# State space steps issued singly between weight pieces, tables through the weight pool, next layer's parameters begun inside the gated unit

## The chip, the cores and the metric

The kernel runs as one program on one core of a Trainium2 chip. Its time is the device time of one execution in microseconds (us), as the median of several executions. The core's engines run side by side and meet only through semaphores: TensorE (PE) does the matrix products, VectorE (DVE), ScalarE (ACT) and GpSimd (POOL) do elementwise work, and SyncE (SP) issues nearly all of this kernel's DMA transfers, in one queue, in program order. Every engine works through its own instructions strictly in order, so an instruction that waits holds up all that stand behind it on that engine.

## The reference

The input is one sequence of 512 positions with 2048 features. Two layers of the same kind follow one another and then a third block of another kind (a gated delta rule beside a sliding window attention), which the change does not touch. One of the first two layers, cut to what matters:

```python
mod = c_act @ w_ada[l] + b_ada[l]                  # 6144 numbers: shift, scale, gate
h = rms_norm(x, norm_g[l]) * (1 + scale) + shift
u, z_s, q, k, v, z_a = split(h @ w_in[l])
y_s = s5_mixer(u, ...) * silu(z_s)
y_a = diff_attention(rope(q), rope(k), v, ...) * silu(z_a)      # 8 heads, two score maps each
x = x + gate * (concatenate([y_s, y_a]) @ w_out[l])

def s5_mixer(u):                                   # 64 groups of 16 channels, 64 complex states each
    a_bar = exp(lam * step); b_bar = (a_bar - 1) / lam * b_mat
    states = scan(a_bar, b_bar @ u)                # linear recurrence over the 512 positions
    y = gelu(real(c_mat @ states) + d_skip * u)
    ab = y @ w_glu + b_glu
    return ab[:, :1024] * sigmoid(ab[:, 1024:])
```

All data are fp32.

## The kernel before, in words

**Weights.** Every weight comes in pieces of 128 x 1024 fp32 (512 KB). `piece` (lines 258 to 274) loads one into a slot of the pool `rawp`, which has five; ACT rounds it into a `hi` part (L266) and `raw - hi` becomes the `lo` part (L269), each in a pool of three slots. `mm3` multiplies in three passes: hi by the activations' high part (`HH`, L281), hi by their low part (`HL`, L282), lo by the high part (L284). For a 128 x 1024 piece against 512 positions that is 24 matmuls. `group_tok` does the same with the activations as the stationary side (L353 to L355), for the values of the attention. `self.pool` decides which engine makes `lo`: with `pool = 2`, which `layer` sets for the attention heads 2 to 7, every second piece's `lo` is made by GpSimd, otherwise all by DVE.

**Filling in.** `mod` of the coming layer is computed without PE: an "ada" piece of `w_ada` is loaded into a slot of the same five (L531) and DVE multiplies and sums it at once (L517, the "dot"). `piece` adds `self.rate` to a counter and calls `self.fill` for each whole number, so that 0.75 or 1 ada piece goes with each weight piece.

**A layer's stages.** `layer(l)` makes u and the gates z_a; then the values of heads 0 to 3 (`group_tok` over eight pieces); heads 0 to 3 (each two weight blocks of two pieces, for q and k, then `attention`); the values of heads 4 to 7; heads 4 to 7; z_s; the gated linear unit `glu` (16 pieces, 8 pairs m of a gate block and a value block); and the out projection (`woA` by `group` in 8 pieces, then `wo` block by block). The stages begin roughly at 315, 385, 775, 880 and 1060 us for layer 0's values, heads, `glu`, out projection and layer 1, and at 1290 and 1345 us for layer 1's values and heads; the third block fills the time from 1960 us on.

**The state space part.** `ssm_params(l)` is a generator that computes tables from the parameters: `prep` builds powers E for a quarter of the states on DVE (`powmul`, L659 to L661: three tensor_tensor operations for each power and part, up to 128 x 512), `products` (L688) and `turned` (L718) multiply and transpose E on PE and write the tables `FT_d`, `K_d` to DRAM, `carried` builds powers on GpSimd and writes `CA_d`. Layer 1's generator, `par_next`, is stepped during layer 0's out projection: first once after `glu`, then from the third `woA` piece on at each piece and after each `wo` block. `ssm_steps(l)` is a generator of 16 loads of u, 8 steps with the tables `FT` (L806, sixteen 64 x 64 matmuls each), the recurrence on GpSimd (62 steps of four small operations, L818 to L821), and 8 steps with `K_d`, `CA_d` and the states (L844, L846). The FT table of step q is loaded as two 256 KB transfers (L799) into one of two halves of the upper part of A, which also receives the values of heads 4 to 7 later. `layer` steps this generator in runs: in layer 0 four steps after the first values and then 4, 4 and 5 in heads 0 and 1; in layer 1 5 and 4 in head 0; and one step after each weight block of heads 4 to 7.

**What sets the order.** The program is written in the order of these calls; a scheduler of the framework then sets each engine's order by priorities and readiness in its own model, and the pools decide which slot an instruction must wait for. `later(600)` gives the recurrence a later priority. DMAs stand in SP's queue in the scheduled order: a load whose slot is still in use holds all later loads.

Of the kernel before, what the change touches and what calls it, by code (L numbers as in the profile page):

```python
# [167 lines left out]
class Kern:  # L168
    def __init__(self, ctx, tc, I, O):
# [18 lines left out]
        self.turn = self.pool = 0  # L188
# [70 lines left out]
    def piece(self, src, n=1024):  # L259
        nc = self.nc  # L260
        self.n_ = getattr(self, "n_", 0) + 1
        raw = self.rawp.tile([128, 1024], F32, tag="raw", name=f"raw_{self.n_}")
        hi = self.hip.tile([128, 1024], F32, tag="hi", name=f"hi_{self.n_}")
        lo = self.lop.tile([128, 1024], F32, tag="lo", name=f"lo_{self.n_}")
        nc.sync.dma_start(raw[:, :n], src)
        nc.scalar.copy(hi[:, :n].bitcast(F32R), raw[:, :n])  # L266
        self.turn = (self.turn + 1) % 4
        eng = nc.gpsimd if self.turn < self.pool else nc.vector
        eng.tensor_tensor(lo[:, :n].bitcast(F32R), raw[:, :n], hi[:, :n], SUB)  # L269
        self.due += self.rate  # L270
# [15 lines left out]
    def blocks(self, srcs, acts, evac, pair=False):  # L286
# [13 lines left out]
        for j, src in enumerate(srcs):  # L300
            ps = self.bank()
            for k0 in range(0, nk, 8):
                hi, lo = self.piece(src[:, k0 * 128:(k0 + 8) * 128])
                self.mm3([(ps, slice(k * 128, (k + 1) * 128), acts[k0 + k], k0 + k == 0, k0 + k == nk - 1) for k in range(8)], hi, lo)
            evac(j, ps)
# [268 lines left out]
    def ssm_params(self, l):  # L574
# [77 lines left out]
        sbqs = [t.rearrange("p (k r a c) -> p k r a c", k=2, r=2, a=8) for t in (g[:, 1536:2048], self.sb2)]  # L652
# [10 lines left out]
        def prep(qd):  # L663
            sbq = sbqs[qd % 2]
# [15 lines left out]
            return E, Cb  # L680

        def products(qd, E, Cb):
# [40 lines left out]
        def carried(qd):  # L723

            sbq = sbqs[qd % 2]
# [11 lines left out]
        for qd in range(4):  # L737
            k = products(qd, *made)
            turned(qd, made[0], (0,))
            yield  # L740
            turned(qd, made[0], (1,))
# [4 lines left out]
            carried(qd)  # L746
# [3 lines left out]
    def ssm_param_storage(self):  # L750
# [10 lines left out]
        self.sb2 = self.small(512, "sb2")  # L761
# [21 lines left out]
    def ssm_steps(self, l):  # L783
# [12 lines left out]
        for q in range(8):  # L796
            ft = self.A[:, 4 + q % 2 * 2:6 + q % 2 * 2, :].rearrange("p a b -> p (a b)")
            for r in range(2):
                nc.sync.dma_start(ft[:, r * 512:(r + 1) * 512], self.FT_d[l][q, r])  # L799
# [69 lines left out]
    def glu(self, l):  # L869
# [8 lines left out]
        for m in range(8):  # L878
# [11 lines left out]
            self.blocks([wg[m]], acts, ev_a)  # L890
        for m in range(8):
# [103 lines left out]
    def layer(self, l, xsrc, on_x, nxt, after_u=lambda: None, par=iter(()), par_next=iter(())):  # L995
# [33 lines left out]
        self.group_tok(I[f"wv{l}"][0], hacts, 512, lambda t, ps: nc.scalar.copy(va[:, t, :], ps), 0, (beside, lambda: None)[l])  # L1029
        for _ in range((4, 0)[l]):  # L1030
            next(ssm)

        def head(h, vt, side):
            qk = []
            self.pool = 2 if h >= 2 else 0
            for b, n in zip((h, 8 + h), side):
                self.blocks([wi[b]], hacts, lambda j, ps: qk.append(self.rope(ps, "q")))
                for _ in range(n):
                    next(ssm, None)
            self.attention(l, h, qk[0], qk[1], vt)  # L1040
        for h in range(4):
            head(h, va, (((4, 4), (5, 0), (0, 0), (0, 0)), ((5, 4), (0, 0), (0, 0), (0, 0)))[l][h])
        vb = A[:, 4:8, :]
        self.group_tok(I[f"wv{l}"][1], hacts, 512, lambda t, ps: nc.scalar.copy(vb[:, t, :], ps))
        for h in range(4, 8):
            head(h, vb, (1, 1))
        for _ in ssm:
            pass
        self.pool = 0
# [14 lines left out]
        self.glu(l)  # L1064
        self.rate = (1, 1)[l]
        next(par_next, None)
# [12 lines left out]
        wait = iter((0, 0))  # L1079
        self.group([I[f"woA{l}"]], [4], yacts, ev_o, side=lambda: next(par_next, None) if next(wait, 1) else None)  # L1080
# [617 lines left out]
```

## Time and profile before

| | us |
|---|---|
| median of 3 executions (3540.87 to 3544.72) | 3542.14 |
| the profiled execution | 3540.92 |
| its span in the trace | 3538.8 |
| PE busy in that span | 3373.7 |
| DVE busy | 2121.2 |
| ACT busy | 1184.6 |
| GpSimd busy | 631.2 |

The trace covers one execution. Busy time is time in which an engine works on an instruction; idle time has a releaser, which is the event that ended it. Only idle time of the engine that sets the end counts. The table of stretches gives, beside the busy times, the clock that TensorE was granted as a share of full speed: after a pause the engine starts again at the lower of its two levels (1.2 GHz instead of 2.4 GHz), and matmuls then start about twice as far apart. DMA share is the mean busy share of the core's 16 DMA engines.

### The profile page before, as it was taken

To read this page: it belongs to the slowest core of one execution; us is meant where nothing else is said; L and a number is where in the kernel's file an instruction comes from. 1 tells how busy PE (TensorE), PEld (TensorE's weight loads), DVE (VectorE), ACT (ScalarE), POOL (GpSimd) and SP (SyncE) were. 2 spreads that over 40 slices of the span, in tenths; PEclk is the share of its full clock that TensorE was granted. 3 is DMA by queue.
4 is the path that set the end of the run, shared out by engine and by line. 5 is a ranking of instruction groups with operands and counts; after the bars stand their busy time and mean duration, and the time that the engine had idled before them with its cause. 6 is when DMAs were issued, how large, how long until landed. Compare 5 with 4: busy or idle time off the path is not lost.

```text
span 3538.8 us, 45321 instructions
## 1 busy us (share of the span) xinstructions
PE 3373.7 (95%) x16541; PEld 2699.5 (76%) x16541; DVE 2121.2 (60%) x4108; ACT 1184.6 (33%) x2044; POOL 631.2 (18%) x885
## 2 busy tenths in 40 slices
PE   7988989999789998899999998999999999999999
PEld 4867767778669876677788887788888877688887
DVE  7994655677957435646575588933893265434432
ACT  3422332353224322323433344222522244433311
POOL 0083591001830004920001202000200000000000
PEclk9999999999899999999999999999999999999999
DMA  9848436656666855356567636233333232224442
GB/s 333 301 155 227 155 117 185 187 186 210 200 215 221 231 172 164 111 174 183 176 220 232 203 118 133 100 107 93 104 96 115 94 107 75 75 99 139 143 140 90
DMA packets 265116, 565.02 MB, mean 160 GB/s; under 512 B 76732, under 2 KB 113853, under 8 KB 264893
## 3 DMA queue, kind: packets, MB, share of 16 engines
q1 hardware_dynamic: 264894, 562.14, 50.2%
q8 instruction: 130, 2.13, 0.2%
q14 instruction: 92, 0.75, 0.1%
HBM read 497.89 MB, written 50.50 MB: 155 GB/s over the span
## 4 chain that ended last, share of the span: by engine, by line
PE 66%; DVE 10%; DMA 10%; POOL 8%; issue 3%; SPq 2%; ACT 1%; DVEq 0%; POOLq 0%; ACTq 0%
PE pp L282 18%; PE pp L281 18%; PE pp L284 18%; DMA raw<-in_wada 6%; DVE lo L269 2%; PE sc L918 2%; DVE G L249 2%; POOL misc L818 1%; POOL G L821 1%; POOL misc L820 1%; POOL misc L819 1%; DVE raw L517 1%; POOL lo L269 1%; POOL G L661 1%; PE pp L353 1%
## 5 line engine op out<-in xcount | busy, mean ns | idle before, releaser
L281 PE MATMUL pp<-HH,hi 128*128 128x512 f32 (+1 forms) x3568 | 1390.5, 393 | 29.5 <-ACT HH L567 18.4
L282 PE MATMUL pp<-HL,hi 128*128 128x512 f32 (+1 forms) x3440 | 1336.5, 392 | 3.2 <-DVE HL L252 3.2
L266 ACT CAST hi<-raw 128x1024 fp32r<-128x1024 f32 (+1 forms) x538 | 560.1, 1043 | 1173.4 <-PE pp L282 918.7
L284 PE MATMUL pp<-HH,lo 128*128 128x512 f32 (+1 forms) x3568 | 904.4, 391 | 8.9 <-DVE lo L269 8.9
L269 DVE TENSOR_TENSOR lo<-raw,hi 128x1024 fp32r<-128x1024 f32 (+1 forms) x506 | 623.6, 1234 | 356.2 <-PE pp L284 183.5
L281 PEld LDWEIGHTS pp<-HH,hi 128*128 128x128 f32 x3568 | 676.3, 190 | 183.3 <-issue 30.0
L284 PEld LDWEIGHTS pp<-HH,lo 128*128 128x128 f32 x3568 | 658.7, 189 | 162.1 <-issue 20.0
L282 PEld LDWEIGHTS pp<-HL,hi 128*128 128x128 f32 x3440 | 651.9, 190 | 152.6 <-issue 22.5
L517 DVE CUSTOM_DVE_ANT_0 raw<-raw,cs,mod 128x1024 f32<-128x1024 f32 x112 | 154.9, 1383 | 245.7 <-DMA raw<-in_wada 243.0
L517 DVE CUSTOM_DVE_ANT_0 raw<-raw,cs,vec 128x1024 f32<-128x1024 f32 x112 | 153.0, 1366 | 231.5 <-DMA raw<-in_wada 224.8
L217 ACT ACTIVATE p<-p,st 128x128 f32<-128x128 f32 (+2 forms) x192 | 101.9, 531 | 201.1 <-DVE st L244 200.9
L1652 POOL TENSOR_TENSOR rp<-rp,n 128x512 f32<-128x512 f32 (+1 forms) x43 | 59.0, 1385 | 430.9 <-ACT n L1651 430.9
L354 PE MATMUL pp<-lo,HH 128*128 128x512 f32 (+1 forms) x320 | 121.7, 385 | 4.1 <-DVE lo L269 4.1
L353 PE MATMUL pp<-hi,HH 128*128 128x512 f32 (+1 forms) x320 | 121.1, 384 | 4.6 <-ACT HH L567 3.1
L269 POOL TENSOR_TENSOR lo<-raw,hi 128x1024 fp32r<-128x1024 f32 x32 | 78.2, 2443 | 263.0 <-PE pp L284 171.9
L355 PE MATMUL pp<-hi,HL 128*128 128x512 f32 (+1 forms) x320 | 115.4, 381 | 0.0
L818 POOL TENSOR_TENSOR misc<-misc,G 128x64 f32<-128x64 f32 x124 | 57.1, 461 | 310.7 <-ACT G L808 301.5
L918 PE MATMUL sc<-rp,rp 64*128 64x128 f32 (+3 forms) x256 | 92.3, 492 | 9.6 <-DVE st L920 9.6
L282 PE MATMUL pp<-A,hi 128*128 128x512 f32 x256 | 100.7, 393 | 0.0
L920 DVE CUSTOM_DVE_ANT_0 p<-sc,cst 128x128 f32<-128x128 f32 (+3 forms) x128 | 61.1, 484 | 39.3 <-PE sc L918 39.0
L1101 POOL TENSOR_TENSOR wt<-n,wt 128x512 fp32r<-128x512 f32 x16 | 24.7, 1545 | 321.4 <-ACT wt L1100 168.7
L354 PEld LDWEIGHTS pp<-lo,HH 128*128 128x128 f32 x320 | 62.5, 196 | 18.7 <-DVE lo L269 5.8
(327 smaller groups left out, 3911.6 us busy)
## 6 DMA issues: line engine op xcount, KB each, us to landing
raw<-in_wada SPq DMA_DIRECT2D x224, 512.0 KB, 4.1
raw<-in_w SPq DMA_DIRECT2D x164, 512.0 KB, 3.6
raw<-in_win SPq DMA_DIRECT2D x128, 512.0 KB, 5.0
raw<-in_wo SPq DMA_DIRECT2D x80, 512.0 KB, 4.6
G<-in_wad SPq DMA_DIRECT2D x64, 512.0 KB, 6.1
raw<-in_wv SPq DMA_DIRECT2D x32, 512.0 KB, 3.7
raw<-in_wglu SPq DMA_DIRECT2D x32, 512.0 KB, 4.5
raw<-in_wuA SPq DMA_DIRECT2D x18, 512.0 KB, 4.7
```

The source lines that it names most:

```text
L217: i = self.nc.scalar.activation(out, src, func, **kw)
L266: nc.scalar.copy(hi[:, :n].bitcast(F32R), raw[:, :n])
L269: eng.tensor_tensor(lo[:, :n].bitcast(F32R), raw[:, :n], hi[:, :n], SUB)
L281: mm(out, hi[:, sl], mh, start=first, stop=False)
L282: mm(out, hi[:, sl], ml, start=False, stop=False)
L284: mm(out, lo[:, sl], mh, start=False, stop=last)
L353: mm(pss[t][:, :n], mh[:, ts], hi[:, sl], start=first, stop=False)
L354: mm(pss[t][:, :n], mh[:, ts], lo[:, sl], start=False, stop=False)
L355: mm(pss[t][:, :n], ml[:, ts], hi[:, sl], start=False, stop=last)
L517: self.nc.vector.tensor_tensor_reduce(w, w, cs, 1.0, self.vec[:, o:o + 1] if first else m, MUL, ADD, m)
L818: T(s1, a8[:, 0], prev, MUL)
L918: nc.tensor.matmul(sc[:, :W], q[rows, i * 128:(i + 1) * 128], k[rows, :W], start=True, stop=True)
```

## The change

1. **No lo parts on GpSimd.** `self.pool` and `self.turn` go; `piece` makes every `lo` on DVE. This concerns 32 pieces, 16 in each of the two layers, in heads 2 to 7.
2. **State space steps singly.** `blocks` gets a callback `side` after each piece. In layer 0, the counts `(8, 1, 2, 2, 2, 2)` are the steps after the first six pieces of heads 0 and 1 (before: 4 after the values, then 4, 4, 5 after blocks). In layer 1, one step is issued after each of the eight pieces of the first values, which are the eight FT steps, and one (the recurrence) after the first piece of head 0 (before: none beside the values, then 5 and 4 in head 0). Heads 4 to 7 keep one step after each block.
3. **FT tables through the pieces' pool.** An FT step takes a slot of the five raw slots and loads its table with one 512 KB transfer, in place of the two halves in A.
4. **Layer 1's parameters begun in the gated unit.** `glu` gets a callback `beside`, which steps `par_next` after m = 1, 3, 4, 5 and 6; the step after `glu` goes, and in `woA` only the fourth and the eighth piece step it (before: the third to the eighth). The slice of inputs `sbq` moves to the pool `rp` (four slots, shared with rope's tiles) from two fixed places, so `sb2` goes.

The diff, cut to its core:

```diff
@@ piece
-        self.turn = (self.turn + 1) % 4
-        eng = nc.gpsimd if self.turn < self.pool else nc.vector
-        eng.tensor_tensor(lo[:, :n].bitcast(F32R), raw[:, :n], hi[:, :n], SUB)
+        nc.vector.tensor_tensor(lo[:, :n].bitcast(F32R), raw[:, :n], hi[:, :n], SUB)
@@ blocks
-    def blocks(self, srcs, acts, evac, pair=False):
+    def blocks(self, srcs, acts, evac, pair=False, side=lambda: None):
...
+                side()
             evac(j, ps)
@@ ssm_params, prep
-            sbq = sbqs[qd % 2]
+            sbq = self.t2("rp", 4).rearrange("p (k r a c) -> p k r a c", k=2, r=2, a=8)
@@ ssm_steps
-            ft = self.A[:, 4 + q % 2 * 2:6 + q % 2 * 2, :].rearrange("p a b -> p (a b)")
-            for r in range(2):
-                nc.sync.dma_start(ft[:, r * 512:(r + 1) * 512], self.FT_d[l][q, r])
+            ft = self.raw()
+            nc.sync.dma_start(ft.rearrange("p (r c) -> p r c", r=2), self.FT_d[l][q].rearrange("r p c -> p r c"))
@@ glu
-    def glu(self, l):
+    def glu(self, l, beside):
...
             self.blocks([wg[m]], acts, ev_a)
+            if m in (1, 3, 4, 5, 6):
+                beside()
@@ layer
-        self.group_tok(I[f"wv{l}"][0], hacts, 512, ..., 0, (beside, lambda: None)[l])
-        for _ in range((4, 0)[l]):
-            next(ssm)
+        self.group_tok(I[f"wv{l}"][0], hacts, 512, ..., 0, (beside, lambda: next(ssm))[l])
+        steps = iter(((8, 1, 2, 2, 2, 2), (1,))[l])
+        def side():
+            for _ in range(next(steps, 0)):
+                next(ssm)
...
-            self.pool = 2 if h >= 2 else 0
...
-        self.glu(l)
-        next(par_next, None)
+        self.glu(l, lambda: next(par_next, None))
...
-        wait = iter((0, 0))
-        self.group([I[f"woA{l}"]], [4], yacts, ev_o, side=lambda: next(par_next, None) if next(wait, 1) else None)
+        turns = iter((0, 0, 0, 1) * 2)
+        self.group([I[f"woA{l}"]], [4], yacts, ev_o, side=lambda: next(turns) and next(par_next, None))
```

After the change `mm3`'s lines are L278, L279 and L281, the products' L685, the transposes' L715, the FT matmuls' L801, the recurrence's L813 to L816, `powmul`'s L656 to L658, the lo part's L266, the dot's L515, the loads' L264 (weights), L529 (ada) and L794 (FT).

**GpSimd in layer 0's heads.** The engine's own order in the middle of the recurrence, before (`lo_3674` is the low part of a weight piece):

```order
L818 TENSOR_TENSOR misc<-misc,G_90 128x64
L819 TENSOR_TENSOR misc<-misc,G_90 128x64
L820 TENSOR_TENSOR misc<-misc,G_90 128x64
L269 TENSOR_TENSOR lo_3674<-raw_3672,hi_3673 128x1024
L821 TENSOR_TENSOR G_90<-misc 128x64
L818 TENSOR_TENSOR misc<-misc,G_90 128x64
```

and after:

```order
L813 TENSOR_TENSOR misc<-misc,G_90 128x64
L814 TENSOR_TENSOR misc<-misc,G_90 128x64
L815 TENSOR_TENSOR misc<-misc,G_90 128x64
L816 TENSOR_TENSOR G_90<-misc 128x64
L813 TENSOR_TENSOR misc<-misc,G_90 128x64
```

The low part no longer stands between the steps of the recurrence, and no step stands ahead of it.

**SP at layer 1's first values and head 0.** The queue of loads before, from the second piece of head 1 on (`in_win`; the values' pieces `in_wv` stand ten to twenty rows further up, the first four FT halves some ninety):

```order
L265 DMA raw_11138<-in_win 128x1024
L531 DMA raw_11144<-in_wada 128x1024
L799 DMA A_86<-FT_d_134 128x512
L265 DMA raw_11182<-in_win 128x1024
L531 DMA raw_11188<-in_wada 128x1024
L265 DMA raw_11215<-in_win 128x1024
L531 DMA raw_11221<-in_wada 128x1024
L799 DMA A_86<-FT_d_134 128x512
L901 DMA rp_10488<-rp_10487 32x512 x4
L799 DMA A_86<-FT_d_134 128x512 x3
```

and after, from the first piece of the values on:

```order
L264 DMA raw_10168<-in_wv 128x1024
L794 DMA raw_10199<-FT_d_134 128x2x512
L264 DMA raw_10219<-in_wv 128x1024
L529 DMA raw_10225<-in_wada 128x1024
L794 DMA raw_10252<-FT_d_134 128x2x512
L264 DMA raw_10272<-in_wv 128x1024
L529 DMA raw_10278<-in_wada 128x1024
L794 DMA raw_10305<-FT_d_134 128x2x512
```

Each table now has a place directly behind a piece of the values, and takes a raw slot there. PE's order in the same place, before, where the end of the first table's matmuls and the second table stand behind head 0's second piece (`lo_10456`):

```order
L282 MATMUL pp_10423<-HL,hi_10455 128x512
L284 MATMUL pp_10423<-HH,lo_10456 128x512 x8
L806 MATMUL sc_10500<-G_90,A_86 64x64 x7
L806 MATMUL sc_10520<-G_90,A_86 64x64 x16
L281 MATMUL pp_10598<-HH,hi_10600 128x512
```

and after, where the second table stands between two pieces of the values:

```order
L352 MATMUL pp_10167<-lo_10221,HH 128x512
L353 MATMUL pp_10167<-hi_10220,HL 128x512
L801 MATMUL sc_10254<-G_90,raw_10252 64x64 x16
L351 MATMUL pp_10164<-hi_10273,HH 128x512
L352 MATMUL pp_10164<-lo_10274,HH 128x512
```

**PE in layer 0's gated unit and out projection.** Before, the first products of layer 1's parameters stand at the end of the eight `woA` pieces (`lo_7467` is the last of them), the next piece being `wo`'s first:

```order
L284 MATMUL pp_7071<-HH,lo_7467 128x512
L284 MATMUL pp_7072<-HH,lo_7467 128x512
L688 MATMUL sc_7172<-G_90,p_7065 32x128 x4
L718 MATMUL tr_7191<-cst,G_90 128x128 x2
L688 MATMUL sc_7172<-G_90,p_7065 32x128 x12
L718 MATMUL tr_7191<-cst,G_90 128x128 x2
L718 MATMUL tr_7199<-cst,G_90 128x128 x4
L281 MATMUL pp_7551<-HH,hi_7553 128x512
```

After, they stand behind the twelfth of the sixteen pieces of `glu` (`lo_6945`), with `glu`'s thirteenth behind them:

```order
L279 MATMUL pp_6942<-HL,hi_6944 128x512
L281 MATMUL pp_6942<-HH,lo_6945 128x512 x8
L685 MATMUL sc_6769<-G_90,p_6620 32x128 x4
L715 MATMUL tr_6788<-cst,G_90 128x128 x4
L715 MATMUL tr_6796<-cst,G_90 128x128 x4
L685 MATMUL sc_6769<-G_90,p_6620 32x128 x12
L695 MATMUL sc_6769<-cst,p_6786 128x128 x2
L715 MATMUL tr_6876<-cst,G_90 128x128 x4
L715 MATMUL tr_6884<-cst,G_90 128x128 x4
L278 MATMUL pp_7041<-HH,hi_7043 128x512
```

DVE makes the E that these products read; its end there, before (`n_7038` and `n_7039` are `prep(0)`'s, `n_7304` is `prep(1)`'s):

```order
L660 TENSOR_TENSOR G_90<-G_90 128x8x64
L517 ISA raw_7692,mod_101<-raw_7692,cs,mod_101 128x1024
L517 ISA mod_101 128x1
L269 TENSOR_TENSOR lo_7554<-raw_7552,hi_7553 128x1024
L661 TENSOR_TENSOR G_90<-G_90,n_7038 128x8x64
L661 TENSOR_TENSOR G_90<-G_90,n_7039 128x8x64
L661 TENSOR_TENSOR G_90<-G_90,n_7304 128x8x64
```

and after (`n_6593` and `n_6594` are `prep(0)`'s):

```order
L657 TENSOR_TENSOR G_90<-G_90 128x8x64
L266 TENSOR_TENSOR lo_7080<-raw_7078,hi_7079 128x1024
L657 TENSOR_TENSOR G_90<-G_90 128x8x64
L515 ISA raw_7156,mod_101<-raw_7156,cs,mod_101 128x1024
L515 ISA mod_101 128x1
L656 TENSOR_TENSOR n_6980<-G_90 128x512
L656 TENSOR_TENSOR n_6981<-G_90 128x512
L657 TENSOR_TENSOR G_90<-G_90 128x8x64
L658 TENSOR_TENSOR G_90<-G_90,n_6593 128x8x64
L658 TENSOR_TENSOR G_90<-G_90,n_6594 128x8x64
L266 TENSOR_TENSOR lo_7117<-raw_7115,hi_7116 128x1024
```

On PE the first products move up by twelve pieces' worth of matmuls (four of `glu`, eight of `woA`). On DVE E's last operations move up by less: counted from the start of `glu`, 11 low parts, 10 dots, 4 gate multiplications (L252), 4 products with it (L249) and 2 operations of prep(1) (L661) that stood ahead of E's end stand behind it now.

## Rows read from the trace of the kernel before

**Rows 1.** The page: busy time of each engine, share of the span, instructions.

```profile
PE 3373.7 (95%) x16541; PEld 2699.5 (76%) x16541; DVE 2121.2 (60%) x4108; ACT 1184.6 (33%) x2044; POOL 631.2 (18%) x885
```

**Rows 2.** Stretches: length, busy us of PE, PEld, DVE, ACT, POOL, clock, DMA share, GB/s.

```profile
400.00:580.00 180.00, 164.48 (x763) 123.70 (x763) 98.86 (x242) 53.20 (x141) 130.62 (x256) 0.96 0.42 128
...
880.00:1060.00 180.00, 148.03 (x754) 119.21 (x754) 135.50 (x208) 39.63 (x56) 109.50 (x105) 0.91 0.67 211
...
1260.00:1375.00 115.00, 99.68 (x642) 80.45 (x641) 41.34 (x53) 26.99 (x33) 1.86 (x3) 0.96 0.55 175
1375.00:1580.00 205.00, 188.69 (x888) 141.73 (x887) 116.21 (x293) 66.53 (x179) 141.23 (x259) 0.96 0.43 134
...
1960.00:3538.00 1578.00, 1547.93 (x7456) 1266.85 (x7455) 865.43 (x1588) 539.16 (x815) 83.70 (x99) 0.99 0.35 112
```

**Rows 3.** PE's waits, 330 to 800 us: total us, times, longest.

```profile
PE tr L938 <- DVE wt L933: 10.9, 3, 6.3
PE sc L806 <- DMA A<-FT_d: 8.9, 1, 8.9
```

**Rows 4.** PE in order of time behind layer 1's FT wait: start us, us.

```profile
1350.24 0.63 PE L281 MATMUL pp<-HH,hi 128*128 128x512 f32 x1
1350.67 0.63 PE L282 MATMUL pp<-HL,hi 128*128 128x512 f32 x1
...
1351.93 0.39 PE L281 MATMUL pp<-HH,hi 128*128 128x512 f32 x1
1352.16 0.40 PE L282 MATMUL pp<-HL,hi 128*128 128x512 f32 x1
```

**Rows 5.** GpSimd's groups by form, 395 to 760 us (layer 0's heads).

```profile
L269 POOL TENSOR_TENSOR lo<-raw,hi 128x1024 fp32r<-128x1024 f32 x15 | 36.6, 2438 | 108.4 <-PE pp L284 50.9 <-ACT wt L933 24.4 <-issue 24.1
L818 POOL TENSOR_TENSOR misc<-misc,G 128x64 f32<-128x64 f32 x62 | 29.6, 477 | 7.3 <-ACT G L808 2.7
```

**Rows 6.** SP's waits, 395 to 760 us.

```profile
SPq L531 <- POOL misc L818: 11.0, 1, 11.0
```

**Rows 7.** DVE's waits, 395 to 760 us.

```profile
DVE raw L517 <- DMA raw<-in_wada: 70.2, 24, 11.1
```

**Rows 8.** PE's waits, 1375 to 1760 us (layer 1's heads).

```profile
PE sc L918 <- DVE st L920: 9.6, 2, 9.3
PE tr L938 <- DVE wt L933: 3.1, 1, 3.1
```

**Rows 9.** PE's waits, 1180 to 1375 us (layer 1's values, head 0).

```profile
PE sc L806 <- DMA A<-FT_d: 11.2, 1, 11.2
PE pp L354 <- DVE lo L269: 4.1, 4, 2.3
```

**Rows 10.** PE's waits, 880 to 1060 us (layer 0's out projection).

```profile
PE sc L688 <- DVE G L661: 20.8, 4, 13.2
PE pp L284 <- DVE lo L269: 8.2, 4, 4.3
PE pp L281 <- DVE A L252: 3.0, 1, 3.0
```

**Rows 11.** PE in order of time: `glu`'s thirteenth piece begins.

```profile
842.15 0.39 PE L281 MATMUL pp<-HH,hi 128*128 128x512 f32 x1
```

**Rows 12.** Table of stretches, from `glu`'s start to E's last operation.

```profile
775.50:926.30 150.80, 134.28 (x593) 109.37 (x591) 125.54 (x256) 44.56 (x55) 49.02 (x53) 0.96 0.64 208
```

**Rows 13.** DVE's groups by form, 775.5 to 926.3 us.

```profile
L269 DVE TENSOR_TENSOR lo<-raw,hi 128x1024 fp32r<-128x1024 f32 x24 | 30.8, 1283 | 0.0
L517 DVE CUSTOM_DVE_ANT_0 raw<-raw,cs,mod 128x1024 f32<-128x1024 f32 x15 | 21.5, 1436 | 20.7 <-DMA raw<-in_wada 20.7
...
L661 DVE TENSOR_TENSOR G<-G,n 128x512 f32<-128x512 f32 x3 | 4.9, 1678 | 0.0
```

**Rows 14.** DVE in order of time, just ahead of E's last operations.

```profile
921.15 2.05 DVE L269 TENSOR_TENSOR lo<-raw,hi 128x1024 fp32r<-128x1024 f32 x1
```

**Rows 15.** GpSimd in order of time, at the same moment.

```profile
918.65 3.46 POOL L659 TENSOR_TENSOR wt<-G 128x512 f32<-128x512 f32 x2
```

More of the change, by code (lines that the diff above doesn't have):

```diff
@@ L187, in __init__ @@
         self.fill, self.rate, self.due = None, 0, 0
-        self.turn = self.pool = 0
         self.act_set, self.act_run = None, []
@@ L651, in ssm_params @@
         T, V = nc.gpsimd.tensor_tensor, nc.vector.tensor_tensor
-        sbqs = [t.rearrange("p (k r a c) -> p k r a c", k=2, r=2, a=8) for t in (g[:, 1536:2048], self.sb2)]
         def powmul(T, tm, out, f, src, n, qd, op=ADD):
@@ L679, in prep, with products @@
                 nc.gpsimd.tensor_copy(Cb[rows, :, :, h, :], sbq[rows, 1])
-            return E, Cb
-        def products(qd, E, Cb):
+            return E, Cb, sbq
+        def products(E, Cb):
             kp = self.sbank("sc", 2)
@@ L721, in turned, with carried @@
                     nc.sync.dma_start(self.FT_d[l][qd * 2 + a0 // 4, r], ft)
-        def carried(qd):
-            sbq = sbqs[qd % 2]
+        def carried(qd, sbq):
             sc = self.t2("wt", 1, shape=(128, 1280))
@@ L737, in ssm_params @@
         for qd in range(4):
-            k = products(qd, *made)
-            turned(qd, made[0], (0,))
+            E, Cb, sbq = made
+            k = products(E, Cb)
+            turned(qd, E, (0,))
             yield
-            turned(qd, made[0], (1,))
+            turned(qd, E, (1,))
             lags(qd, *k)
@@ L745, in ssm_params @@
                 made = prep(qd + 1)
-            carried(qd)
+            carried(qd, sbq)
             yield
@@ L760, in ssm_param_storage @@
         self.u_d = self.dp.tile([1024, 512], F32, name="u_d")
-        self.sb2 = self.small(512, "sb2")
     def ssm_pad(self):
@@ L1028, in beside, with head @@
                 next(ssm)
-        self.group_tok(I[f"wv{l}"][0], hacts, 512, lambda t, ps: nc.scalar.copy(va[:, t, :], ps), 0, (beside, lambda: None)[l])
-        for _ in range((4, 0)[l]):
-            next(ssm)
-        def head(h, vt, side):
-            qk = []
-            self.pool = 2 if h >= 2 else 0
[L1036 to L1039, printed above, removed]
+        self.group_tok(I[f"wv{l}"][0], hacts, 512, lambda t, ps: nc.scalar.copy(va[:, t, :], ps), 0, (beside, lambda: next(ssm))[l])
+        steps = iter(((8, 1, 2, 2, 2, 2), (1,))[l])
+        def side():
+            for _ in range(next(steps, 0)):
+                next(ssm)
+        def head(h, vt, after=0):
+            qk = []
+            for b in (h, 8 + h):
+                self.blocks([wi[b]], hacts, lambda j, ps: qk.append(self.rope(ps, "q")), side=side)
+                if after:
+                    next(ssm)
             self.attention(l, h, qk[0], qk[1], vt)
         for h in range(4):
-            head(h, va, (((4, 4), (5, 0), (0, 0), (0, 0)), ((5, 4), (0, 0), (0, 0), (0, 0)))[l][h])
+            head(h, va)
         vb = A[:, 4:8, :]
@@ L1045, in layer @@
         for h in range(4, 8):
-            head(h, vb, (1, 1))
+            head(h, vb, 1)
         for _ in ssm:
             pass
-        self.pool = 0
         for t in range(8):
```

## The prediction

> **What bounds the kernel now.** I read the page's busy times first: PE is busy 95% of the span [rows 1], so the time can only fall by what PE waits for, 165 us in all, and by what its clock loses after waits. Then the table of stretches [rows 2], to see where these 165 us lie. The third block (from 1960 us) has 30 us of them in 1578 us, and nothing of it is edited. The rest of the waits that the change can reach lies in four stretches: layer 0's heads (180 − 164.5 = 15.5 us, 400 to 580), layer 0's end of `glu` and out projection (180 − 148.0 = 32.0 us), layer 1's values and start of head 0 (115 − 99.7 = 15.3 us) and layer 1's heads (205 − 188.7 = 16.3 us); a single FT wait of 8.9 us stands just ahead of layer 0's heads [rows 3]. Between these stretches PE is busy to within a few us, and so the kernel is as long as PE's stream plus these waits. Then PE's waits by stretch, which name the releasers. Last PE in order of time behind a wait: matmuls start 0.43 us apart, later 0.23 us [rows 4]. This stretch at the lower of the two clock levels lasts some eight matmuls, so that a wait of over 3 us costs about 8 × 0.20 = 1.6 us more.
>
> **The change part by part.** The sum is made against the profiled execution (3540.9 us, of which 3538.8 are the span).
>
> *A, layer 0's FT tables.* PE waits 8.9 us, once, for a table in A [rows 3]; with the clock 10.5 us. The cause is in SP's queue: a half of A is free only when the step before last has been multiplied, and its load then stands behind weight loads that wait for their own slots. With the raw slots a table is asked for as early as a weight piece is. What remains is that eight tables now share five slots with the weights, in a run of eight steps behind one piece: I leave 2.5 us for that. Gain 8, between 5 and 10.5.
>
> *B, layer 0's heads.* The largest wait there is for DVE's copies in the attention (10.9 us in 3 [rows 3]). DVE is not short of time: it is busy 99 of 180 us [rows 2]. It stands in order behind the dot, which waits 70.2 us in all for ada loads, once 11.1 [rows 7]. The ada load waits in SP's queue for a raw slot whose last reader is a low part on GpSimd, and that stands in the recurrence: one such wait of SP is 11.0 us [rows 6]. There GpSimd makes 15 low parts of 2.44 us (36.6 us) among 62 × 4 operations of about 0.45 us [rows 5]. After the change no low part is on GpSimd, so a slot is freed at DVE's pace; the recurrence is shorter by about ten low parts (24 us), which also brings the states' loads forward. The price: 16 low parts at about 1.28 us (the mean in [rows 13]), 20 us more on DVE in nearly 400 us, in a stretch where it is busy 55%; that is covered by PE's stream as long as the dot doesn't wait. Of 15.5 us and three clock losses (5) I take 15, keeping 5 for the states' loads and for a low part that comes late; between 6 (only the longest wait goes) and 20.
>
> *C, layer 0's `glu` and out projection.* PE waits 20.8 us in 4 for E (L661), of which 13.2 once, and 11.2 us in 5 for low parts and A [rows 10]; with some six clock losses of 1.6 the stretch loses about 42. The first products move up 65 us in PE's stream: they come when PE gets to `glu`'s thirteenth piece, at 842.2 on the clock of before [rows 11]. DVE must have E by then. From `glu`'s start to E's end DVE is busy 125.5 of 150.8 us [rows 12]. From that go 11 low parts (11 × 1.28 = 14.1), 10 dots (10 × 1.3 = 13; their mean is 1.44 where they collide most) and the ten small operations that now stand behind, about 11 (L661 at 1.68, the rest about 1): 38 in all, 36 to 40. So 775.5 + 87.5 = 863, and some of the 25 us that DVE idled on ada loads [rows 12, 13] is still there: I take 4, and E at 867 (range 848, if E is limited by the last piece alone, to 875). PE then waits 867 − 842 = 25 us at one place, with the clock 27. The later products and the low parts that were late at 924 to 1033 have twelve pieces' more time, and I leave 1 to 5 us for the third and fourth. So 42 − 28 = 14, between 0 and 30. This is the most uncertain term. No row of before shows how soon DVE gets to E when it is asked for earlier.
>
> The Trainium skill ("SBUF — State Buffer", section "Who interferes with whom") says that a DVE instruction with two inputs in SBUF and a GpSimd instruction that reads SBUF share a port pair which one holds for its whole instruction while the other blocks. The trace agrees: a low part took 2.05 us against a mean of 1.28 [rows 13, 14] while GpSimd was in a tensor_tensor [rows 15]. By the rule the change helps in the heads and not in `glu`, where `carried` on GpSimd again runs beside `prep` on DVE; with every operation of prep at the slow row's price E would come at the late end, 875, and the sum would be 8 us higher.
>
> *D, layer 1's values.* PE waits 4.1 us for low parts [rows 9], since DVE does load, dot and low part of one piece after the other. An FT table in between makes a piece longer for PE (16 small matmuls, about 1 us) and for the loads (512 KB more). Gain 3, between −4 and 4.
>
> *E, layer 1's FT tables.* One wait of 11.2 us [rows 9] and its clock loss, 12.8. The tables were written long before, and their loads now go with the pieces of the values, where no wait is long. Gain 12, between 9 and 13.
>
> *F, layer 1's heads.* As B: 9.6 us for a statistic on DVE, 3.1 for its copies [rows 8], 16.3 us in all and 5 for the clock. Gain 16, between 6 and 21.
>
> *What costs nothing.* `sbq` in `rp`'s slots is two loads earlier or later at the start, where the loads are the limit: ±3 us at the most. Two more changes of ACT's function table (Sin between sigmoids) stand on ACT, which is idle two thirds of the time.
>
> Sum: 8 + 15 + 14 + 3 + 12 + 16 = 68. 3540.9 − 68 = 3472.9; the median of before is 1.2 us above the profiled execution, so 3474 us. Bounds added as independent give ±20.
>
> **The rivals.** R1: E isn't earlier. DVE keeps its order of before, the dots wait for loads in the gated unit, and E comes near 885: PE then waits 43 us where it has nothing else, and C loses nothing or gains nothing (42 − 46 = −4). 3540.9 − 54 + 4 = 3491, with the median 3492. For it: DVE is the engine that is waited for throughout this stretch, and PE's wait of 13.2 came although the products stood 65 us later. Against: over half of what stood ahead of E is removed.
>
> R2: the raw slots are crowded. The 16 tables take slots of the five; where weight, ada and table go through the same slots, weights come late. If this costs A and D wholly, and 2 us at half of the tables of E, then 8 + 3 + 12 = 23 go, and with some more late low parts 3500.
>
> R3: the low parts on DVE bring the waits of B and F back, since DVE works in order and gets 41 us more (32 × 1.28), all ahead of attention work. Then B and F give 31 less: 3505.
>
> R4, slower: SP is stopped by the tables. A table's load waits for a slot that only PE's matmuls or a dot frees, and all loads behind it wait too; PE then waits once for each table. DVE's waits for ada loads, in the same ring, are 70.2/24 = 2.9 us each [rows 7]; with 1.6 for the clock 4.5 us a table, 16 × 4.5 = 72. Then A, D and E (23) are lost and 72 − (the rest, 45) = 27 us more: 3569. It is slower than before from a wait of 1.2 us a table on (16 × 2.8 = 45). Against: PE's matmuls of a table take 1 us, so that a slot is held shortly, and the DMA engines are busy 42 to 55% in the heads and values [rows 2].
>
> That the change doesn't do what it says can be left out for the low parts (none is on GpSimd in the new order), but not for the tables: in layer 0 the first FT matmul still stands at the place in PE's order where it stood.
>
> **How the numbers follow.** My forecast, all terms about as above (3446 to 3500): 0.55. R1: 0.18. R2: 0.10. R3: 0.09. R4 and other things that cost more than 68: 0.05. A small rest (0.03) lies within 0.2% of before, where several of R1 to R3 come together. A measurement of this kernel can tell about 0.2% (7 us) from no change. Faster by over 0.2%: 0.92, within 0.03, slower 0.05. The range reaches from 3444 (C near its best end, B and F whole) to 3508 (R3 included).
>
> **What would show it.** In the profile after: no FT wait over 3 us near 350 and 1335; SP no longer waits for GpSimd's recurrence, and DVE's dots wait well under 70 us in layer 0's heads; PE busy over 95% in both heads stretches. PE's longest wait is one for E (L658) at L685 near 820 (A and B being gained ahead of it), of 18 to 30 us, with the waits of the out projection nearly gone. The prediction is wrong if that wait is short (under 10 us: time below 3460), if it comes several times over 15 us, or if PE waits for low parts or weights (L278, L281) in the values or heads.

## The result, and the profile after

The changed kernel takes 3572.31 us (median of 4 runs, 3570.81 to 3574.41) against 3541.51 us before: a ratio of 1.0092, 95% interval 1.008 to 1.0105. It is slower by 31 us, where 68 us less were forecast. The profiled execution has a span of 3570.5 us.

The page of the changed kernel, busy times, answers to [rows 1]: PE does the same work, so all that came is waiting.

```profile
PE 3373.6 (94%) x16541; PEld 2701.5 (76%) x16541; DVE 2135.7 (60%) x4140; ACT 1182.1 (33%) x2045; POOL 568.9 (16%) x853
```

The table of stretches after (columns as in [rows 2]); the stretches are the same times, in which a little other work lies by now:

```profile
200.00:300.00 100.00, 78.85 (x428) 63.34 (x426) 79.95 (x127) 25.20 (x36) 86.17 (x84) 0.90 0.53 154
400.00:580.00 180.00, 155.59 (x795) 118.68 (x794) 104.66 (x252) 55.96 (x157) 111.64 (x248) 0.91 0.44 136
...
880.00:1060.00 180.00, 156.21 (x752) 126.86 (x753) 110.63 (x136) 44.75 (x61) 79.99 (x86) 0.92 0.63 200
1260.00:1375.00 115.00, 115.00 (x717) 93.78 (x716) 46.37 (x56) 32.00 (x39) 5.74 (x12) 1.00 0.63 214
1375.00:1580.00 205.00, 183.33 (x843) 138.84 (x842) 124.35 (x292) 63.15 (x168) 113.16 (x237) 0.94 0.44 139
```

PE's waits after, 120 to 2000 us (in all, times, longest), answer to [rows 3], [rows 8], [rows 9] and [rows 10]:

```profile
PE sc L685 <- DVE G L658: 27.2, 5, 12.6
PE tr L935 <- DVE wt L930: 20.0, 4, 16.9
PE tr L927 <- DVE p L251: 18.9, 7, 13.3
PE sc L685 <- POOL p L676: 12.1, 1, 12.1
...
PE pp L278 <- DVE A L251: 8.6, 2, 8.2
```

No matmul waits for an FT table any more, and layer 1's values and head 0 run without a wait (115.00 of 115.00 us busy). That part came as forecast. But the heads of both layers have new single waits of 16.9 and 13.3 us, and there is a wait of 12.1 us for GpSimd at layer 0's parameters. Where the time came from is seen best by taking the same matmul in both traces: the first or the last of the four groups of values (the only matmuls with the activations stationary), and the first of a stage, found by counting the weights' matmuls. The changed kernel is later by:

| at | us later | added in this part |
|---|---|---|
| layer 0, end of the first values | 14.2 | 14 (parameters) |
| layer 0, end of the second values | 25.9 | 12 (heads 0 to 3, second values) |
| layer 0, start of `glu` | 19.1 | −7 (heads 4 to 7, z_s) |
| layer 1, start of the first values | 41.3 | 22 (`glu`, out projection) |
| layer 1, end of the first values | 45.6 | 4 (8 us of FT matmuls lie here now) |
| layer 1, start of head 2 | 27.0 | −19 (no FT wait, no FT matmuls) |
| layer 1, start of the second values | 17.9 | −9 (heads 2 and 3) |
| layer 1, end of the second values | 31.6 | 14 (second values) |
| end | 31.7 | 0 |

The largest part, 22 us, lies in `glu` and the out projection. What stands behind the two waits in the heads is one row of SP's waits in each layer (395 to 600 us, and 1400 to 1620 us):

```profile
SPq L834 <- POOL G L816: 20.8, 1, 20.8
```

```profile
SPq L834 <- POOL G L816: 21.4, 1, 21.4
```

L834 is the load of the recurrence's states, G L816 the recurrence's last operation. In the new order this load stands ahead of the next weight and ada loads in SP's queue. DVE in order of time shows what follows in layer 1: the dot's data are late by the time for which SP stood, and the attention's operations stand behind the dot.

```profile
1485.17 0.17 DVE L921 RECIPROCAL st<-st 128x2 f32<-128x2 f32 x1
1503.41 1.28 DVE L515 CUSTOM_DVE_ANT_0 raw<-raw,cs,vec 128x1024 f32<-128x1024 f32 x1 [18.08 <-DMA raw<-in_wada]
```

In layer 0 DVE itself also stands before the recurrence's last step, with an operation of the third block on the small tile `misc`, which the recurrence uses too, and the copy that PE waits for stands right behind it:

```profile
540.86 0.31 DVE L243 TENSOR_SCALAR misc<-rep 128x32 f32<-128x32 f32 x1 [20.54 <-POOL misc L814]
541.09 0.28 DVE L930 COPY wt<-tr 128x128 f32<-128x128 f32 x1
```

### The profile page after: what moved, and what is told of

Read it like the earlier page. It is cut to its first block, busy times and chain, and to the rows that moved or that the text cites. A ratio compares the mean times of both kernels' runs of the same rounds, so it can differ in the third digit from the quotient of the medians.

```text
span 3570.5 us, 45261 instructions
## 1 busy us (share of the span) xinstructions
PE 3373.6 (94%) x16541; PEld 2701.5 (76%) x16541; DVE 2135.7 (60%) x4140; ACT 1182.1 (33%) x2045; POOL 568.9 (16%) x853
## 4 chain that ended last, share of the span: by engine, by line
PE 65%; DVE 10%; DMA 10%; POOL 8%; issue 3%; SPq 2%; ACT 1%; DVEq 0%; ACTq 0%; POOLq 0%
PE pp L278 17%; PE pp L279 17%; PE pp L281 17%; DMA raw<-in_wada 4%; DVE lo L266 2%; POOL misc L813 2%; POOL G L816 2%; POOL misc L815 2%; POOL misc L814 1%; DMA raw<-in_win 1%; DVE G L248 1%; DMA G<-in_wad 1%; PE sc L915 1%; DVE raw L515 1%; PE pp L351 1%
## 5 line engine op out<-in xcount | busy, mean ns | idle before, releaser
L278 PE MATMUL pp<-HH,hi 128*128 128x512 f32 (+1 forms) x3568 | 1391.4, 393 | 44.3 <-ACT HH L565 21.7
L279 PE MATMUL pp<-HL,hi 128*128 128x512 f32 (+1 forms) x3440 | 1336.3, 392 | 2.9 <-DVE HL L251 2.9
L266 DVE TENSOR_TENSOR lo<-raw,hi 128x1024 fp32r<-128x1024 f32 (+1 forms) x538 | 663.8, 1235 | 418.8 <-ACT hi L265 196.9
L281 PE MATMUL pp<-HH,lo 128*128 128x512 f32 (+1 forms) x3568 | 899.7, 390 | 7.7 <-DVE lo L266 7.7
L278 PEld LDWEIGHTS pp<-HH,hi 128*128 128x128 f32 x3568 | 676.7, 190 | 198.8 <-issue 32.9
L281 PEld LDWEIGHTS pp<-HH,lo 128*128 128x128 f32 x3568 | 660.4, 189 | 155.8 <-issue 14.9
L279 PEld LDWEIGHTS pp<-HL,hi 128*128 128x128 f32 x3440 | 652.4, 190 | 153.2 <-issue 23.8
L515 DVE CUSTOM_DVE_ANT_0 raw<-raw,cs,mod 128x1024 f32<-128x1024 f32 x112 | 149.9, 1338 | 235.7 <-DMA raw<-in_wada 235.6
L515 DVE CUSTOM_DVE_ANT_0 raw<-raw,cs,vec 128x1024 f32<-128x1024 f32 x112 | 146.0, 1303 | 200.2 <-DMA raw<-in_wada 193.4
L813 POOL TENSOR_TENSOR misc<-misc,G 128x64 f32<-128x64 f32 x124 | 64.8, 523 | 368.6 <-ACT G L803 359.1
L279 PE MATMUL pp<-A,hi 128*128 128x512 f32 x256 | 100.7, 393 | 0.0
L351 PEld LDWEIGHTS pp<-hi,HH 128*128 128x128 f32 x320 | 62.3, 195 | 16.3 <-ACT HH L565 3.9
L251 DVE SCALAR_TENSOR_TENSOR p<-pp,vec,p 128x511 f32<-128x511 f32 (+3 forms) x88 | 65.4, 743 | 13.3 <-ACT p L216 10.8
```

The costliest lines, as they stand in the source:

```text
L266: nc.vector.tensor_tensor(lo[:, :n].bitcast(F32R), raw[:, :n], hi[:, :n], SUB)
L278: mm(out, hi[:, sl], mh, start=first, stop=False)
L279: mm(out, hi[:, sl], ml, start=False, stop=False)
L281: mm(out, lo[:, sl], mh, start=False, stop=last)
L351: mm(pss[t][:, :n], mh[:, ts], hi[:, sl], start=first, stop=False)
L515: self.nc.vector.tensor_tensor_reduce(w, w, cs, 1.0, self.vec[:, o:o + 1] if first else m, MUL, ADD, m)
```

## The experiments

Four kernels each do one part of the change alone; together they are the change.

**One: low parts on DVE only.**

```diff
-        eng.tensor_tensor(lo[:, :n].bitcast(F32R), raw[:, :n], hi[:, :n], SUB)
+        nc.vector.tensor_tensor(lo[:, :n].bitcast(F32R), raw[:, :n], hi[:, :n], SUB)
```

> The kernel before with one part of the change: all low parts on DVE, none on GpSimd. The prediction's theory (terms B and F): the low parts in the recurrence free raw slots late, so the waits of the heads go and the time falls by 20 to 31 us, to 3511 to 3522. The rival, from the trace of the changed kernel: SP's queue and DVE stop for the end of the recurrence (for the states' loads and for an operation on the same tile) wherever the order puts these, with or without low parts; then the waits only change their place and the time is 3535 to 3555, and SP waits for the recurrence's last operations in one piece of 10 us or more.

3549.4 us against 3539.5 us for the kernel before on the same chip, ratio 1.0028 (1.0016 to 1.0039). The rival held. SP's waits in layer 0's and layer 1's heads:

```profile
SPq L837 <- POOL G L819: 23.8, 1, 23.8
```

```profile
SPq L837 <- POOL G L819: 28.9, 1, 28.9
```

and PE's waits, 120 to 2000 us:

```profile
PE tr L946 <- DVE n L249: 15.6, 1, 15.6
PE tr L928 <- DVE A L252: 14.9, 1, 14.9
```

Before, SP's waits for GpSimd in these stretches were several, the longest 11.0 us [rows 6] and 12.4. The row of layer 1 in the kernel before (1400 to 1620 us):

```profile
SPq L531 <- POOL misc L818: 14.5, 2, 12.4
```

Without the low parts they are one long one for the states' load.

**Two: steps singly, tables through the raw slots.** The diff of `ssm_steps`, `blocks` and the heads as in the change.

> The kernel before with the second and third part of the change: state space steps singly, tables through the raw slots; low parts on GpSimd, parameters and their inputs' slots as before. The prediction's theory (A, D, E): 23 us less, 3519. The rival: layer 1 gains its 14 us (no wait for a table or a low part between 1270 and 1350 us), but in layer 0 the last tables come only between the first heads' pieces, the recurrence begins some 20 us later (420 instead of 398) and the states' loads stop SP: that part costs 5 to 15 us, and the time is 3530 to 3545.

3544.1 us, ratio 1.0011 (1.0 to 1.0023): inside the rival's range. Layer 1's first values and head 0 lose their waits, but head 0 then has one of 9.3 us for rope's result; the recurrence in layer 0 starts at 404.3 us, 6 us late and not 20 as the rival had it. By the trace layer 0 loses 5 us between the first values and `glu`; layer 1 is 9 us ahead at head 2 and has given that back by its own `glu`. The interval reaches down to no change.

**Three: parameters begun in `glu`.**

> The kernel before with the fourth part alone: layer 1's parameters begun in the gated unit, the inputs' slices in their two old places. The prediction's theory (C): one wait of about 25 us for E, else little: 14 us less, 3528. The rival, from the trace of the changed kernel: the first wait is only 12 us, but ACT and DVE stop for a p slot behind a table's write, the out projection's evacuations stand behind dots, and the later products wait again: 10 to 20 us more, 3552 to 3562.

3544.5 us, ratio 1.0015 (1.0005 to 1.0024). Neither range held it: it is a loss of 5 us, between them. PE's waits, 780 to 1080 us:

```profile
PE sc L688 <- DVE G L661: 18.2, 2, 16.9
PE pp L281 <- DVE A L252: 11.2, 1, 11.2
```

The waits for E fell by only 2.6 us against [rows 10]. The one for the out projection's evacuation grew from 3.0 to 11.2 us. DVE in order of time in that kernel shows why: the evacuation (L252) stands behind dots that wait for their loads one after the other.

```profile
940.68 1.28 DVE L517 CUSTOM_DVE_ANT_0 raw<-raw,cs,mod 128x1024 f32<-128x1024 f32 x1 [2.51 <-DMA raw<-in_wada]
...
945.43 1.29 DVE L517 CUSTOM_DVE_ANT_0 raw<-raw,cs,mod 128x1024 f32<-128x1024 f32 x1 [2.32 <-DMA raw<-in_wada]
...
950.59 1.28 DVE L517 CUSTOM_DVE_ANT_0 raw<-raw,cs,mod 128x1024 f32<-128x1024 f32 x1 [2.73 <-DMA raw<-in_wada]
951.80 0.08 DVE L517 DVE_READ_ACCUMULATOR2_ANT mod<- 128x1 f32 x1
951.80 1.41 DVE L252 SCALAR_TENSOR_TENSOR A<-pp,mod,A 128x512 f32<-128x512 f32 x2
```

**Four: `sbq` in the pool rp.**

> The kernel before with the inputs' slices (sbq) in the pool rp alone. The prediction put this at nothing (3 us either way): 3539 to 3545. The rival, from the start of the changed kernel: DVE's operations for the next quarter of layer 0's parameters follow without a gap, GpSimd is kept out for 12 us at about 243 us and the third products come late: 8 to 12 us more, 3550 to 3554.

3549.1 us, ratio 1.0032 (1.0021 to 1.0043). The size is the rival's, the place is not: only 2 us of it lie ahead of the end of layer 0's first values, 3 more in layer 0's heads. Singly the four parts cost 9.9, 4.6, 5.0 and 9.6 us, 29 in all, against 31 for the change. That the sum fits so well is partly chance, since by stage they don't add: parameters +14 in the change, and 2, 0 or less in each part.

**Five: the change with `sbq` in its old places.**

> The changed kernel with one part undone: the inputs' slices (sbq) again in their two fixed places, all else changed. Theory 1 (the slices' four slots let prep run ahead on DVE, which keeps GpSimd out at the start, and crowd the gated unit): the changed kernel's 14 us at the start (until the end of layer 0's first values) go wholly and part of the 15 us in the gated unit: 3546 to 3556 (changed kernel: 3572). Theory 2 (the 14 us at the start come from the tables' loads and steps, not from sbq): 3565 to 3572.

3551.06 us, 21 us below the changed kernel. At the end of layer 0's first values the 14.2 us are 2.1. Experiment four lost 2.2 us there. So the loss at the start needs `sbq` in the pool together with another part of the change; no run shows which. GpSimd in order of time in the changed kernel, and then in this one, shows the same two operations of `carried` on 128 x 256:

```profile
243.20 12.58 POOL L656 TENSOR_TENSOR wt<-G 128x256 f32<-128x256 f32 x2
```

```profile
245.51 1.82 POOL L658 TENSOR_TENSOR wt<-G 128x256 f32<-128x256 f32 x2
```

In the kernel before they took 6.86 us:

```profile
242.30 6.86 POOL L659 TENSOR_TENSOR wt<-G 128x256 f32<-128x256 f32 x2
```

**Six: the change with the states' loads, and the third block's operation on `misc`, on GpSimd.**

```diff
-                    nc.sync.dma_start(s2[64 * r:64 * r + 64, h], Sv[64 * h:64 * h + 64, r, q * 4:q * 4 + 4, :])
+                    nc.gpsimd.dma_start(s2[64 * r:64 * r + 64, h], Sv[64 * h:64 * h + 64, r, q * 4:q * 4 + 4, :])
...
-        self.ts(v3(al), self.rep[:, 0:8].unsqueeze(1).to_broadcast([128, 4, 8]), 1.0)
+        nc.gpsimd.tensor_scalar(v3(al), self.rep[:, 0:8].unsqueeze(1).to_broadcast([128, 4, 8]), 1.0, None, MUL)
```

> The changed kernel with the loads of the recurrence's states (s<-G) issued by GpSimd behind its recurrence instead of SP, and the third block's operation on the same small tile as the recurrence also on GpSimd instead of DVE. Theory 1 (SP's queue and DVE stop for the recurrence's end, 20 us each layer): the two long waits of PE in the heads (16.9 and 13.4 us) go, also what is queued behind them: 25 to 34 us less, 3538 to 3547. Theory 2 (PE's waits there come from the low parts on DVE and its attention work; SP's wait is beside the point): less than 10 us, 3562 or more.

3529.0 us, 43 us below the changed kernel and below the kernel before (ratio 0.9972, 0.9962 to 0.9981). It is even more than theory 1 gave. By the traces (44 us apart) half of it lies in the heads, where the states' loads stand: 6 us in layer 0 from the end of the first values to `glu`, and 16 in layer 1 from head 2 on. Another 6 us lie ahead of that, at the start, and 16 in layer 0's `glu` and out projection, where no load of the states stands. There the scheduler's order is another one in this kernel; that this makes the 16 us was not tried by itself. Its stretch of layer 1's heads:

```profile
1375.00:1580.00 205.00, 199.22 (x932) 148.54 (x932) 138.58 (x338) 68.56 (x188) 99.97 (x197) 0.99 0.50 155
```

PE waits there 6 us in place of the 22 us of the changed kernel. Of layer 0's long wait one is left at the matmul that reads the states; PE comes to it at 539.3 us and the recurrence ends at 546.5 (PE's waits, 395 to 2000 us):

```profile
PE sc L841 <- issue: 10.8, 1, 10.8
```

**Seven and eight: the kernel before with layer 1's steps and tables alone, without and with the edit of six.**

```diff
+            if l:
+                ft = self.raw()
...
-        self.group_tok(..., 0, (beside, lambda: None)[l])
+        self.group_tok(..., 0, (beside, lambda: next(ssm))[l])
```

> The kernel before with the state space steps singly beside the first values and tables through the raw slots in layer 1 alone. Theory 1 (in layer 1 this part is a gain, and layer 0 took it back in the run with both layers, 3544): 3526 to 3535. Theory 2 (layer 1's gain is given back in its own heads, since the recurrence is then elsewhere against the weights' loads): 3537 to 3545.

3533.2 us, ratio 0.9987 (0.9977 to 0.9997), inside theory 1's range: in layer 1 the part is a gain of about 6 us.

> As the run before in this list (layer 1 alone), with the states' loads and the operation on the recurrence's tile on GpSimd as in the second of this list; low parts still partly on GpSimd. Theory 1: what SP loses behind the recurrence's end goes as well, 8 to 20 us below the kernel before: 3519 to 3532. Theory 2: with low parts on GpSimd in between, SP waits for these anyway, and it is within 4 us of the run without: 3526 to 3545.

3541.75 us, ratio 1.0006 (0.9996 to 1.0016). Theory 1 had it lower than the run without, theory 2 within 4 us of it; it is 8.5 us above, with intervals that overlap a little. So with low parts still on GpSimd, whose queue they then share with the states' loads, the edit of six is no gain. It also speaks against a gain from fewer issues in SP's queue alone. Where the 8.5 us lie isn't settled: the two profiled spans differ by 3.4 us only (3538.4 and 3535.0), in small shares in several stages.

**Nine to eleven: the two costs together, and without the parts that gain nothing.** Nine is five with the edit of six; ten is nine with the parameters begun after `glu` as before; eleven is ten with layer 0's steps and tables as before.

> The changed kernel with the states' loads and the operation on the recurrence's tile on GpSimd, and with the inputs' slices (sbq) again in their two fixed places. Theory 1 (two separate costs: SP and DVE behind the recurrence, 43 us by the run with that mended; sbq, 21 us by the run with that undone; they add): 3505 to 3513. Theory 2 (the two shift the same waits): 3520 to 3530.

3508.6 us, ratio 0.9932 (0.9912 to 0.9951). The two costs add. Against the kernel before on the same chip the change stands at +30.8 us, five at +11.8 and six at −10.3, so that the two are worth 19.0 and 41.1; 30.8 − 60.1 = −29.3, and −28.2 were measured.

> The kernel of the run before in this list with layer 1's parameters begun as before, after the gated unit. Theory 1 (the earlier products cost what they cost alone, 5 us, as they cost from layer 0's second values' end to layer 1 in the traces): 5 to 10 us below the run before in this list. Theory 2 (they are a gain once the other two costs are gone): 5 us or more above it.

3505.9 us, ratio 0.9915 (0.99 to 0.9929), the fastest of all, 31 us below the kernel before. It is 2.6 us below nine, less than theory 1 said and with overlapping intervals: the earlier parameters are no gain that can be seen.

> As the run before in this list, with layer 0's steps and tables as in the kernel before (only layer 1's through the raw slots); all low parts on DVE, the states' loads and the operation on the recurrence's tile on GpSimd. Theory 1 (layer 0's tables through the raw slots are no gain, since the recurrence starts later): 0 to 8 us below the run before in this list. Theory 2 (A of the prediction is a gain of 8 in layer 0 too): 5 to 10 us above it.

3510.6 us, ratio 0.9928 (0.9909 to 0.9946). That is 4.7 us above ten, short of theory 2's range and against theory 1, but with overlapping intervals: layer 0's tables through the raw slots gain or cost less than the runs show.

**Twelve: the change with only the operation on `misc` on GpSimd.**

> The changed kernel with only the third block's operation on the recurrence's tile moved to GpSimd; the states' loads stay on SP. Theory 1: in layer 0 DVE no longer stops for 20 us, but SP still does, as in layer 1, where DVE had no such operation and PE waited 13 us; PE's wait of 16.9 us falls little, and the time by 0 to 6 us, 3566 to 3572. Theory 2: the operation on DVE is the cause in layer 0, SP's wait there is beside the point: 14 to 18 us less, 3554 to 3558.

3578.4 us, ratio 1.0119 to the kernel before (1.0104 to 1.0134), where the whole change has 1.0092: no gain, rather a loss, so neither range held it. SP's wait in layer 0 stays, and PE's wait only changes its place (SP's waits 395 to 600 us; PE in order of time):

```profile
SPq L834 <- POOL G L816: 25.7, 1, 25.7
```

```profile
559.86 1.01 PE L839 MATMUL sc<-A,G 128*64 128x128 f32 x4 [15.54 <-DMA A<-K_d]
```

DVE now waits for an ada load in place of GpSimd, as in layer 1:

```profile
564.94 1.28 DVE L515 CUSTOM_DVE_ANT_0 raw<-raw,cs,mod 128x1024 f32<-128x1024 f32 x1 [24.74 <-DMA raw<-in_wada]
```

So SP's stop costs as much by itself, and taking away the operation on DVE alone gains nothing. What that operation costs where SP does not stop was not measured: the loads were never moved without it.

## Why the prediction was wrong

*A* (8 forecast). The wait for a table in layer 0 went as said: from 8.9 us to none. The price was elsewhere: the last tables lie between the pieces of the first heads, and with the 14 us from the start the recurrence begins at 420.3 us instead of 398.2. Before and after:

```profile
398.21 0.35 POOL L818 TENSOR_TENSOR misc<-misc,G 128x64 f32<-128x64 f32 x1 [2.69 <-ACT G L808]
```

```profile
420.25 0.35 POOL L813 TENSOR_TENSOR misc<-misc,G 128x64 f32<-128x64 f32 x1 [105.90 <-ACT G L803]
```

*B and F* (15 and 16 forecast). Layer 0 lost 5 us from the end of the first values to `glu`, where A and B were to gain 23; layer 1 lost 5 from head 2 to the end, where F was to gain 16. The step that failed is "a slot is freed at DVE's pace", with its help that the shorter recurrence "also brings the states' loads forward". The slots were freed so, but SP did not come to use them. The states' loads stand ahead of the recurrence's end in SP's queue in either case, and then everything behind them waits: 20.8 and 21.4 us, where the sum kept 5 for the states' loads and a late low part together. Before, the low parts on GpSimd held the same queue, in several shares. Taking them away without moving the states' load changed which instruction stops SP, and made it one long stop: before, with shares of up to 12 us, PE's longest waits in these heads were 6.3 and 9.3 us, and with one of 21 they are 16.9 and 13.3. Experiments one and six show it from both sides, and twelve shows that the other suspect, the operation on `misc`, is not needed for it. The recurrence became shorter by 11 us in layer 0 (132 to 121) and not by 24: only seven low parts stood inside it (17.6 us) and not ten, and its own operations took 6 us more in all (L813 at 522 ns against 477 for L818 [rows 5]).

*C* (14 forecast; 5 lost alone, 22 in the change). This step failed too, and by more than B or F. The wait for E was 16.9 us alone, 12.6 in the change after a wait of 5.2 for a low part, where 25 were said: E came earlier than the sum had it. What failed is the other half of the term, that the waits for A and low parts would vanish. The dots, in order on DVE, wait for loads whether or not prep's work is gone, and the evacuation behind them became later (8.2 us in the change). In the change the third products waited 7.4 us, which had not waited before, the fourth 6.7 (7.3 before), and ACT stood once for a slot of the pool `p`, whose last reader was a table's write in SP's queue:

```profile
902.34 0.58 ACT L717 COPY p<-tr 128x512 f32<-128x512 f32 x1 [14.94 <-DMA FT_d<-p]
```

That write stood behind one of `CA_d`, whose data GpSimd had yet to make, and for which SP stopped 13.7 us (SP in order of time, and its waits from 780 to 1080 us):

```profile
897.02 1.09 SPq L730 DMA_DIRECT2D CA_d<-G  x2
898.20 2.00 SPq L718 DMA_DIRECT2D FT_d<-p  x2
```

```profile
SPq L730 <- POOL G L658: 18.5, 2, 13.7
```

It is the pattern of the heads once more: a transfer that stands ahead of the end of its producer. The longest stop at this line was 3.2 us before and is 5.8 in experiment six, which lost 6 us in this stage and not 22. But twelve, with 9.1, lost 22 us as well, and three and nine, with 9.3, lost 4 and 3. No run moves these writes by themselves, so how much of the 22 us is theirs stays open.

*D and E* (15 forecast) were right: no wait is left in layer 1's values and head 0, and from the first values to head 2 the change gained 14 us. Seven gains less (6 us): in its trace 13 us are gained by head 2, and about as many are given back in the heads that follow.

*What costs nothing* (±3 us at the start) was wrong by 11 us: with `sbq` in its new place, beside the rest of the change, GpSimd is kept out for longer. I looked at the loads and not at what the new place does to the order of DVE's work. That DVE runs ahead because the two fixed places no longer hold it back is my reading; no row shows it.

*The rivals.* R4 had the side and the engine right, SP stopped with all loads behind, and named the wrong instruction: the tables' loads stop it for 6.9 us at most, the states' for 21. R3 is excluded for layer 1 by six and nine: all low parts are on DVE, and from head 2 on they gain 11 and 16 us. In layer 0 it isn't: of the 23 us of A and B six gained 1 and nine 4, and PE waits 10.8 and 9.9 us there at the matmul that reads the states. R1 and R2 did not occur.

The Trainium skill ("SBUF — State Buffer", section "Who interferes with whom") was weighed with 8 us in C, where E came earlier and not later than the sum had it. Rows that bear on it are those of the start, in the last section.

## What to carry to other kernels

In an in-order DMA queue, ask of every load what its data wait for, not only what its slot waits for: one load that stands ahead of its producer's end stops all loads behind it, and that moves into engines that have nothing to do with it. Issue such a load from the queue of the engine that makes the data, if that queue has no other work that others wait for: with low parts in it, in experiment eight, the same edit gained nothing. When an edit takes instructions out of a chain, look at which instruction is the next to stop the same queue before counting the gain.

## What the runs showed of the hardware

Two GpSimd operations on 128 x 256 took 12.58 us in the changed kernel (243.20 to 255.78), 6.86 in the kernel before and 1.82 in experiment five. One by one in the changed kernel:

```profile
243.20 8.41 POOL L656 TENSOR_TENSOR wt<-G 128x256 f32<-128x256 f32 x1
```

```profile
251.57 4.21 POOL L656 TENSOR_TENSOR wt<-G 128x256 f32<-128x256 f32 x1
```

In these 12.6 us DVE ran without a gap, nearly all of it operations with two inputs in SBUF, and until 255 us at their usual durations. Rows of DVE in the changed kernel:

```profile
243.28 1.20 DVE L266 TENSOR_TENSOR lo<-raw,hi 128x1024 fp32r<-128x1024 f32 x1
...
247.37 0.27 DVE L657 TENSOR_TENSOR G<-G,rp 128x128 f32<-128x128 f32 x1
...
251.06 0.67 DVE L248 TENSOR_TENSOR A<-pp,A 128x512 f32<-128x512 f32 x1
...
255.20 0.72 DVE L657 TENSOR_TENSOR G<-G,rp 128x128 f32<-128x128 f32 x1
```

The first GpSimd operation ended at 251.60, beside a DVE operation that reads one of its inputs from PSUM. The second ended at 255.78, and beside it a DVE operation took 0.72 us where the same had taken 0.27: there DVE was the one that waited. The Trainium skill ("SBUF — State Buffer", section "Who interferes with whom") says that the one which issues first holds the shared ports for its whole instruction while the other blocks. These rows agree, and show more: from 243.3 to 251.0 us, through back-to-back DVE instructions with two inputs in SBUF, GpSimd did not get in. The kernel before shows the same: its first operation ended at 248.59, in the first gap of DVE.

```profile
246.83 1.28 DVE L661 TENSOR_TENSOR G<-G,n 128x512 f32<-128x512 f32 x2
249.02 1.28 DVE L517 CUSTOM_DVE_ANT_0 raw<-raw,cs,vec 128x1024 f32<-128x1024 f32 x1 [0.91 <-DMA raw<-in_wada]
```

It is not always so. In experiment five the two operations ran beside back-to-back instructions of DVE as well, and there DVE's took longer, as this one; an operation of its kind and size took 0.67 us in the changed kernel (at 248.44):

```profile
245.75 1.10 DVE L659 TENSOR_TENSOR G<-G 128x512 f32<-128x512 f32 x1
```

What decides between the two isn't shown, and that the ports are the reason was not tried by itself. What the three kernels show is that the same two operations took from 1.8 to 12.6 us, by how they fell against DVE's. In the changed kernel GpSimd's copy of the third quarter's inputs came later by it, and PE waited 12.1 us for that copy (3.7 in the kernel before).
